# Windowed attention beside a gated scan: normalizing after the value product, reciprocals through the matrix engine, norms for two chunks together

## The chip, the cores and the metric

The kernel runs on one core of a Trainium2 chip. A core has five engines that each work through their own instructions in order and meet at semaphores: TensorE (PE; its weight loads are shown as PEld), VectorE (DVE), ScalarE (ACT), GpSimd (POOL) and SyncE (SP), which here issues most transfers between the device memory and SBUF. Matmul results land in PSUM, which is divided into banks of 512 float32 per partition. The metric is the device time of one execution in microseconds (us); the time shown of the kernel before is the median of three executions. A trace of one further execution was taken by the hardware profiler.

## The reference

One layer of a diffusion backbone: 1024 latent tokens (16 rows of 64) and 256 context tokens, width 1024. After a modulated RMS norm, one input projection feeds two groups:

- group A, a gated DeltaNet with 4 heads of 128, scanned forward and backward in chunks (the kernel takes chunks of 128: 2 of context, then 8 of latent tokens in each direction), then a per-head RMS norm and a gate;
- group B, neighbourhood attention with 8 heads of 64, each latent query over a window of latent keys and all context keys with one softmax.

Both are joined by an output projection, and a SwiGLU feed-forward follows. What the change touches is this much of it:

```python
# group B
s = jnp.concatenate([s_win.reshape(B, H, N_COL_BLK, QB_W, n_win), s_ctx], axis=-1)
p = jax.nn.softmax(s, axis=-1).astype(v.dtype)
o = (jnp.einsum("bhnqic,binchd->bnqhd", p_win, v_r)
     + jnp.einsum("bhnqk,bkhd->bnqhd", p[..., n_win:], v_ctx))
# group A, o_f and o_b from the two scans
o = (o_f + rev(o_b)).transpose(0, 2, 1, 3)
o = rms_norm(o, out_norm_w) * jax.nn.silu(z.astype(jnp.float32))
```

## The kernel before, in words

The kernel runs stage after stage: the modulation, the input projection (with the preparation of the scans' small inverses beside it), then **one stage in which the scans of group A and the attention of group B run interleaved**, then the output projection, the feed-forward's up products (L1313) and its down products (L1654). The change lies in the interleaved stage.

**Attention.** The work is 32 pairs: 4 head pairs (`hp`) x 2 halves of the rows x 4 column blocks. `pair` (L285) handles one: 128 queries of two heads (u = 0, 1) against 640 keys each. It takes a PSUM tile `sc` of three banks, of which two exist, so pair n+2 takes the one of pair n. Step one: the scores (L302, float16 high and low parts, 6 matmuls for u = 0 and 4 for u = 1); VectorE adds the bias tile `bt` and takes the row maximum (L304), negates it (L306), ScalarE takes the exponential with the maximum as bias and sums along the row (L307), VectorE takes the reciprocal of the sum (L308) and scales the 640 probabilities (L309). Step two: 5 transposes per head into `sc` (L314), copied out by ScalarE (L317). Step three: 10 matmuls with the values into columns 1280 to 1407 of `sc` (L324), the two heads on the two halves of the 128 output partitions, each 64 columns of the array; ScalarE copies the product to `out` (L326). `bt` is filled by POOL (zeros for the context, L270) and by a transfer issued on SP (L271), one pair ahead. Each complete `out` is split into a high and a low part by `store` (L365: ScalarE, then POOL L372).

**Scan.** `scan` (L1161) handles one chunk of one direction: matmuls with the state (L1171, L1181), with the inverse (L1190), the attention inside the chunk (L1202) and the state update (L1207), each followed by VectorE or ScalarE work on its result (L1173, L1184, L1187, L1194, L1196, L1203, L1213). Both directions run side by side, 10 rounds. The second direction to reach a latent chunk adds into `oacc` and then runs `finish(c)` (L1222) as the end of its own scan: load z, square sums on ScalarE (L1228), 14 small VectorE operations for the inverse root, four products with z and the root on VectorE (L1235), and, two rounds of its generator later, the transposes of the chunk (`turned`: L1111, L1114, L1115). The chunks that are last in their direction are transposed after the stage, behind the first output-projection matmuls.

**Order.** The work is written as generators. After each step of a live scan generator, `beside(PACE)` (L1246) gives the attention 0.72 of a step. A scheduler then orders each engine's instructions from that program, so matmuls of scan and attention alternate in small groups; on the chip each engine keeps this order. Instructions on different engines that touch the same PSUM bank are kept apart by semaphores.

Of the kernel before, what the change touches and what calls it, by code (L numbers as in the profile page):

```python
# [9 lines left out]
F32 = mybir.dt.float32  # L10
# [3 lines left out]
AF = mybir.ActivationFunctionType  # L14
OP = mybir.AluOpType
# [7 lines left out]
NAH, ND = 8, 64  # L23
# [65 lines left out]
def hybrid(ctx, tc, a, dbg):  # L89
# [37 lines left out]
    ident = M[C_ID]  # L127
# [125 lines left out]
    def attention(nw):  # L253

        def load(hd):
            qs = nw.tile([128, L], F16, name="qs", tag="qs", bufs=4)
            kh = nw.tile([128, T], F16, name="kh", tag="kh", bufs=4)
            kl = nw.tile([128, T], F16, name="kl", tag="kl", bufs=4)
            sp.dma_start(qs, nq_d[hd].rearrange("i d t -> (i d) t"))
            for i in range(2):  # L260
                sp.dma_start(kh[i * 64:i * 64 + 64], nk_d[0, hd])
                sp.dma_start(kl[i * 64:i * 64 + 64], nk_d[1, hd])
            return qs, kh, kl

        def biases(hp, half, cb):

            out = []
            for u, w0 in enumerate(WIN):
                bt = nw.tile([128, 640], F32, name="bt", tag="bt", bufs=4)
                pool.memset(bt[:, CTX[w0]], 0.0)  # L270
                sp.dma_start(bt[:, w0:w0 + 384], a["rpb"][2 * hp + u, half, CASE[cb]])  # L271
                out.append(bt)
            return out

        def values(hp, half, cb):
            vw = nw.tile([128, 3, 128], F32, name="vw", tag="vw", bufs=3)
            sp.dma_start(vw, vw_d[:, hp, cb, half:half + 3])
            return vw

        def context(hp):  # L280
            vc = nw.tile([128, 2, 128], F32, name="vc", tag="vc")
            sp.dma_start(vc, nv_d[0:CT, hp * 128:hp * 128 + 128].rearrange("(c p) d -> p c d", p=128))
            return vc

        def pair(heads, bts, vw, vc, half, cb, out):  # L285

            r0 = 4 * half
            sc = psum[-1].tile([128, 1536], F32, name="sc", tag="sc", bufs=2)
            mx = nw.tile([128, 2, 4], F32, name="mx", tag="mx", bufs=3)
            for u, (head, w0, bt) in enumerate(zip(heads, WIN, bts)):  # L290
                qs, kh, kl = head
                q = qs[:, (half * 4 + cb) * 128:(half * 4 + cb + 1) * 128]
                kv = [kx[:, CT:].rearrange("p (r c) -> p r c", c=64)[:, r0:r0 + 12, BLKS[cb]:BLKS[cb] + 32]
                      for kx in (kh, kl)]
                parts = [(CTX[w0].start, CTX[w0].stop, (kh[:, 0:CT], kl[:, 0:CT]))]
                if w0:
                    parts += [(256, 512, [x[:, 0:8] for x in kv]), (512, 640, [x[:, 8:12] for x in kv])]
                else:
                    parts += [(0, 384, kv)]
                for n0, n1, ks in parts:  # L300
                    for i in range(2):
                        pe.matmul(sc[:, u * 640 + n0:u * 640 + n1], q, ks[i], start=i == 0, stop=i == 1)  # L302
                m = mx[:, u]
                dve.tensor_tensor_reduce(bt, sc[:, u * 640:u * 640 + 640], bt, 1.0, -3.0e38, OP.add, OP.max,  # L304
                                         m[:, 0:1])
                dve.tensor_scalar(m[:, 1:2], m[:, 0:1], -1.0, None, op0=OP.mult)  # L306
                act.activation(bt, bt, AF.Exp, bias=m[:, 1:2], accum_out=m[:, 2:3])  # L307
                dve.reciprocal(m[:, 3:4], m[:, 2:3])  # L308
                dve.tensor_scalar(bt, bt, m[:, 3:4], None, op0=OP.mult)  # L309
            yield 1  # L310
            pts = []
            for u, bt in enumerate(bts):
                for j in range(5):
                    pe.transpose(sc[:, u * 640 + j * 128:u * 640 + (j + 1) * 128],  # L314
                                 bt[:, j * 128:(j + 1) * 128], ident)
                pt = nw.tile([128, 640], F32, name="pt", tag="pt", bufs=3)
                act.copy(pt, sc[:, u * 640:u * 640 + 640])  # L317
                pts.append(pt)
            yield 1
            for j in range(5):  # L320
                for u, (w0, pt) in enumerate(zip(WIN, pts)):
                    vals = [vc[:, i] for i in range(2)] + [vw[:, i] for i in range(3)]
                    vv = (vals[j] if w0 else vals[(j + 2) % 5])[:, u * ND:u * ND + ND]
                    pe.matmul(sc[u * ND:u * ND + ND, 1280:1408], vv, pt[:, j * 128:(j + 1) * 128],  # L324
                              start=j == 0, stop=j == 4)
            act.copy(out.rearrange("p (r b c) -> p r b c", r=8, b=4)[:, :, cb],  # L326
                     sc[:, 1280:1408].rearrange("p (r c) -> p r c", r=8))
            yield 1

        order = [(hp, half, cb) for hp in range(NAH // 2) for half in range(2) for cb in range(4)]  # L330
        heads = {0: [load(0), load(1)]}
        vcs = {0: context(0)}
        bt, vw = biases(*order[0]), values(*order[0])
        yield 1
        old = None
        for n, (hp, half, cb) in enumerate(order):
            if half == 1 and cb in (0, 2) and hp + 1 < NAH // 2:
                heads.setdefault(hp + 1, []).append(load(2 * hp + 2 + cb // 2))
                if cb == 0:
                    vcs[hp + 1] = context(hp + 1)  # L340
            if cb == 0:
                out = nw.tile([128, 512], F32, name="no", tag="no")
            if old:
                next(old)
            cur = pair(heads[hp], bt, vw, vcs[hp], half, cb, out)
            next(cur)
            if n + 1 < len(order):
                bt, vw = biases(*order[n + 1]), values(*order[n + 1])
            yield 1
            if old:  # L350
                next(old)
                if cb == 0:
                    store(*done)
            if cb == 3:
                done = out, hp, half
            old = cur
            yield 1
        next(old)
        yield 1
        next(old)  # L360
        store(*done)
# [755 lines left out]
    with ExitStack() as gs:  # L1117
# [10 lines left out]
        def work(name, bufs=2, dt=F32):  # L1128
            return sw.tile([128, 4, 128], dt, name=name, tag=name, bufs=bufs)
# [31 lines left out]
        def scan(d, c):  # L1161
# [52 lines left out]
                                                 op0=OP.mult, op1=OP.add)  # L1214
                S[d] = sn
            yield 1
            if lat:
                if c in seen:
                    yield from finish(c)
                seen.add(c)  # L1220

        def finish(c):  # L1222
            o = oacc[:, c - 2]
            z, sq = work("z"), work("sq", 1)
            sp.dma_start(fl(z), z_d[(c - 2) * 128:(c - 1) * 128])
            r = sw.tile([128, 4], F32, name="orr", tag="orr")
            for h in range(4):
                act.activation(sq[:, h], o[:, h], AF.Square, accum_out=r[:, h:h + 1])  # L1228
            t = sw.tile([128, 3, 4], F32, name="nwt", tag="nwt")
            dve.tensor_tensor(r, r, RQ2[:, c - 2], OP.mult)  # L1230
            dve.tensor_scalar(t[:, 0], r, 1.0 / DH, EPS, op0=OP.mult, op1=OP.add)
            rsqrt(r, t[:, 0], t[:, 1])
            dve.tensor_tensor(r, r, RQ[:, c - 2], OP.mult)
            for h in range(4):
                dve.scalar_tensor_tensor(o[:, h], o[:, h], r[:, h:h + 1], z[:, h], op0=OP.mult, op1=OP.mult)  # L1235
            if c in last:
                return
            yield 1
            yield 1
            turned(c)  # L1240
            yield 1

        last = [ORDER[0][-1], ORDER[1][-1]]
        count = [0.0]

        def beside(n):  # L1246
            count[0] += n
# [6 lines left out]
        for i in range(NCH):  # L1254
            if i + 1 < NCH:
                for d in range(2):
                    load(d, ORDER[d][i + 1], ORDER[1 - d][i + 2:i + 3])
            live = [scan(d, ORDER[d][i]) for d in range(2)]
            while live:
                nxt = []  # L1260
                for n, g in enumerate(live):
                    if next(g, 0):
                        nxt.append(g)
                    beside(PACE)
                live = nxt
        for _ in fill:
            pass

# [467 lines left out]
```

## Time and profile before

| | |
|---|---|
| time, median of 3 (lowest to highest) | 1556.46 us (1555.35 to 1559.38) |
| profiled execution: its own time | 1557.82 us |
| profiled execution: span from the first to the last instruction | 1556.0 us |
| granted TensorE clock, mean | 0.986 |
| busy PE, DVE, ACT, POOL, share of the span | 95%, 65%, 46%, 15% |
| instructions PE, DVE, ACT, POOL | 8702, 1856, 1376, 280 |
| scan-and-attention stage | about 577 to 823 us |

Busy times are sums over an engine's instructions. Matmuls overlap in the pipeline, so a busy TensorE may still lose time between them. A row of waits names the instruction that waited, what released it, and how long the engine stood idle for it in total, how often, and the longest. A row of groups gives line, engine, operation, tile written and read, shapes and count, then busy us and mean ns of one, then the engine's idle time before them and its releasers. A row of windows gives the busy us of each engine in a stretch, with the granted clock, the share of the DMA engines and their rate.

### The profile page before, as it was taken

How to read it: one execution, taken by the hardware profiler on the slowest of the kernel's cores; microseconds unless marked ns; L12 is line 12 of the kernel's file. 1: busy time of each engine (PE TensorE's matmuls, PEld its weight loads, DVE VectorE, ACT ScalarE, POOL GpSimd, SP SyncE). 2: the span in 40 equal slices, each digit the busy share in tenths (PEclk: the TensorE clock that was granted, in tenths of full speed). 3: DMA queues.
4: the chain of work that ended last, by engine and by line, in shares of the span. 5: the costliest groups of instructions: out<-in, count | busy, mean ns of one | idle time of the engine just before them, and what ended most of it. 6: DMA issues, size and time to landing. Idle time of an engine off the chain costs nothing. (4 is left out here: it accounts for less than half of the span.)

```text
span 1556.0 us, 24056 instructions
## 1 busy us (share of the span) xinstructions
PE 1481.6 (95%) x8702; PEld 1234.4 (79%) x8702; DVE 1003.7 (65%) x1856; ACT 718.5 (46%) x1376; POOL 229.1 (15%) x280
## 2 busy tenths in 40 slices
PE   7999999999889988997999999999999999999998
PEld 4788787679888766886788878888888888888887
DVE  5774496573254655678997559855665656689652
ACT  6442554654353355666763266333333334454440
POOL 1154401633354320111100000000000000000000
PEclk9999999999999999999999999999999999999999
DMA  9274221677355568999736601633323224698742
GB/s 391 59 221 125 72 76 61 204 219 212 122 173 157 167 190 251 283 287 262 213 114 227 233 34 53 227 108 106 104 102 102 102 102 156 229 378 283 241 147 81
DMA packets 202422, 267.35 MB, mean 172 GB/s; under 512 B 16832, under 2 KB 112576, under 8 KB 201280
## 3 DMA queue, kind: packets, MB, share of 16 engines
q1 hardware_dynamic: 196688, 261.07, 52.3%
q10 hardware_dynamic: 5616, 4.76, 0.9%
q8 instruction: 68, 1.11, 0.3%
q14 instruction: 50, 0.41, 0.1%
HBM read 201.02 MB, written 68.94 MB: 173 GB/s over the span
## 5 line engine op out<-in xcount | busy, mean ns | idle before, releaser
L403 PE MATMUL blk<-hh,whi 128*128 128x512 f32 (+1 forms) x410 | 122.4, 393 | 1.4 <-ACT kk L548 1.4
L1374 ACT CAST uhi<-wq 128x512 fp32r<-128x512 f32 x101 | 61.1, 622 | 132.2 <-issue 84.9
L1374 ACT CAST uhi<-ws 128x512 fp32r<-128x512 f32 x91 | 53.9, 621 | 146.7 <-PE ps L1313 92.5
L403 PE MATMUL blk<-hh,wlo 128*128 128x512 f32 (+1 forms) x410 | 117.0, 379 | 0.6 <-POOL wlo L200 0.6
L403 PE MATMUL blk<-hl,whi 128*128 128x512 f32 (+1 forms) x410 | 115.3, 376 | 0.3 <-DVE hl L689 0.3
L1375 DVE TENSOR_TENSOR ulo<-wq,uhi 128x512 fp32r<-128x512 f32 x101 | 67.6, 687 | 58.8 <-ACT uhi L1374 33.7
L1313 PE MATMUL ps<-hT,uhi 128*128 128x512 f32 x336 | 103.7, 390 | 0.0
L1313 PE MATMUL ps<-lT,uhi 128*128 128x512 f32 x336 | 103.5, 389 | 0.0
L1313 PE MATMUL ps<-hT,ulo 128*128 128x512 f32 x336 | 103.4, 389 | 0.0
L1313 PE MATMUL ps<-hB,uhi 128*128 128x512 f32 x288 | 89.2, 391 | 0.6 <-ACT hB L1488 0.6
L1313 PE MATMUL ps<-lB,uhi 128*128 128x512 f32 x288 | 88.8, 389 | 0.4 <-DVE lB L1489 0.4
L1313 PE MATMUL ps<-hB,ulo 128*128 128x512 f32 x288 | 88.6, 389 | 0.0
L586 PE MATMUL blk<-zhi,hh 128*128 128x256 f32 (+1 forms) x288 | 84.7, 294 | 1.1 <-ACT kk L548 1.1
L403 PEld LDWEIGHTS blk<-hh,wlo 128*128 128x128 f32 x410 | 72.5, 192 | 15.6 <-POOL wlo L200 0.9
L403 PEld LDWEIGHTS blk<-hl,whi 128*128 128x128 f32 x410 | 72.5, 193 | 14.8 <-DVE hl L689 0.8
L586 PE MATMUL blk<-zhi,hl 128*128 128x256 f32 (+1 forms) x288 | 83.0, 288 | 0.0
L403 PEld LDWEIGHTS blk<-hh,whi 128*128 128x128 f32 x410 | 69.9, 194 | 16.5 <-issue 4.0
L586 PE MATMUL blk<-zlo,hh 128*128 128x256 f32 (+1 forms) x288 | 81.8, 284 | 0.0
L1313 PEld LDWEIGHTS ps<-lT,uhi 128*128 128x128 f32 x336 | 63.1, 188 | 13.2
L1313 PEld LDWEIGHTS ps<-hT,ulo 128*128 128x128 f32 x336 | 63.1, 188 | 13.1
L1313 PEld LDWEIGHTS ps<-hT,uhi 128*128 128x128 f32 x336 | 62.9, 188 | 12.9
L200 POOL TENSOR_TENSOR wlo<-wraw,whi 128x1024 fp32r<-128x1024 f32 x18 | 44.7, 2484 | 183.8 <-ACT whi L199 164.4
(359 smaller groups left out, 3651.6 us busy)
## 6 DMA issues: line engine op xcount, KB each, us to landing
wq<-w_fo SPq DMA_DIRECT2D x99, 256.0 KB, 4.1
wq<-w_gu SPq DMA_DIRECT2D x88, 256.0 KB, 2.9
wad<-wa SPq DMA_DIRECT2D x64, 256.0 KB, 4.0
bt<-rpb SPq DMA_DIRECT2D x64, 192.0 KB, 3.6
t_d<-g SPq DMA_DIRECT2D x22, 512.0 KB, 3.6
fr<-t_d SPq DMA_DIRECT2D x44, 256.0 KB, 5.1
f_d<-g SPq DMA_DIRECT2D x33, 256.0 KB, 2.1
fr<-f_d SPq DMA_DIRECT2D x33, 256.0 KB, 4.3
```

Of the source, the lines that this page charges most:

```text
L200: lo_engine.tensor_tensor(o, r, h.bitcast(F32), OP.subtract)
L403: pe.matmul(o, ww[:, k], xx[k][:, s], start=k == 0 and j == 0, stop=k == KT - 1 and j == 2)
L586: pe.matmul(p[:, :c1 - c0], x[k][:, s], ww[:, k, c0:c1], start=k == 0 and j == 0, stop=k == KT - 1 and j == 2)
L1313: pe.matmul(o, w[wi][:, k], x[xi][:, k], start=first and k == 0 and j == 0, stop=k == n - 1 and j == 2, skip_group_check=True)
L1374: act.copy(hi, self.raw[key])
L1375: dve.tensor_tensor(lo, self.raw[key], hi.bitcast(F32), OP.subtract)
```

## The change

- **Softmax.** L304 now forms minus (score + bias) and takes the row minimum (the built-in factor is -1), so that the exponential is taken with scale -1 and that minimum as bias, and the negation L306 is gone. The probabilities stay undivided (L309 is gone); one reciprocal per pair covers both heads.
- **The division** comes after the product with the values. Two matmuls per pair, 64 columns wide, take the reciprocals (broadcast along the 64 columns) as weights and the identity as the moving operand, which turns them into rows that lie like the product, in columns 1408 to 1535 of `sc`. ScalarE copies them to `out`, and VectorE multiplies the product from PSUM into `out`, in place of ScalarE's copy L326.
- **The gated norm.** `finish` takes both chunks that ended in a round, and runs as a third generator beside the scans of the next round (after the last round, alone). The small operations work on both chunks at once; except for the last two chunks, POOL multiplies `oacc` with z, and ScalarE scales by the root in place of VectorE's L1235.

```diff
                 m = mx[:, u]
-                dve.tensor_tensor_reduce(bt, sc[:, u * 640:u * 640 + 640], bt, 1.0, -3.0e38, OP.add, OP.max,
+                dve.tensor_tensor_reduce(bt, sc[:, u * 640:u * 640 + 640], bt, -1.0, 3.0e38, OP.add, OP.min,
                                          m[:, 0:1])
-                dve.tensor_scalar(m[:, 1:2], m[:, 0:1], -1.0, None, op0=OP.mult)
-                act.activation(bt, bt, AF.Exp, bias=m[:, 1:2], accum_out=m[:, 2:3])
-                dve.reciprocal(m[:, 3:4], m[:, 2:3])
-                dve.tensor_scalar(bt, bt, m[:, 3:4], None, op0=OP.mult)
+                act.activation(bt, bt, AF.Exp, scale=-1.0, bias=m[:, 0:1], accum_out=m[:, 2:3])
+            dve.reciprocal(mx[:, :, 3], mx[:, :, 2])
             yield 1
...
             yield 1
+            for u in range(2):
+                pe.matmul(sc[u * ND:u * ND + ND, 1408:1536], mx[:, u, 3:4].to_broadcast([128, ND]), ident,
+                          start=True, stop=True)
+            o, av, inv = [x.rearrange("p (r c) -> p r c", r=8) for x in (out, sc[:, 1280:1408], sc[:, 1408:1536])]
+            o = o[:, :, cb * 16:cb * 16 + 16]
+            act.copy(o, inv)
             for j in range(5):
...
-            act.copy(out.rearrange("p (r b c) -> p r b c", r=8, b=4)[:, :, cb],
-                     sc[:, 1280:1408].rearrange("p (r c) -> p r c", r=8))
+            dve.tensor_tensor(o, av, o, OP.mult)
...
-            if lat:
-                if c in seen:
-                    yield from finish(c)
+            if c in seen:
+                ended.append(c)
+            elif lat:
                 seen.add(c)
 
+        def finish(cs):
+            cs = sorted(cs)
+            two = slice(cs[0] - 2, cs[1] - 1, cs[1] - cs[0])
+            os, zs = [oacc[:, c - 2] for c in cs], [work("z") for c in cs]
+            r = sw.tile([128, 2, 4], F32, name="orr", tag="orr")
+            for i, c in enumerate(cs):
+                sp.dma_start(fl(zs[i]), z_d[(c - 2) * 128:(c - 1) * 128])
+                sq = work("sq", 1)
+                for h in range(4):
+                    act.activation(sq[:, h], os[i][:, h], AF.Square, accum_out=r[:, i, h:h + 1])
+            final = cs == sorted(last)
+            if not final:
+                for o, z in zip(os, zs):
+                    pool.tensor_tensor(z, o, z, OP.mult)
+            yield 1
+            t = sw.tile([128, 3, 2, 4], F32, name="nwt", tag="nwt")
+            dve.tensor_tensor(r, r, RQ2[:, two], OP.mult)
             dve.tensor_scalar(t[:, 0], r, 1.0 / DH, EPS, op0=OP.mult, op1=OP.add)
             rsqrt(r, t[:, 0], t[:, 1])
+            dve.tensor_tensor(r, r, RQ[:, two], OP.mult)
+            for i, c in enumerate(cs):
+                for h in range(4):
+                    if final:
+                        dve.scalar_tensor_tensor(os[i][:, h], os[i][:, h], r[:, i, h:h + 1], zs[i][:, h],
+                                                 op0=OP.mult, op1=OP.mult)
+                    else:
+                        act.activation(os[i][:, h], zs[i][:, h], AF.Copy, scale=r[:, i, h:h + 1])
+                yield 1
+            for c in cs:
+                if c not in last:
+                    yield 1
+                    turned(c)
...
-            live = [scan(d, ORDER[d][i]) for d in range(2)]
+            live = [scan(d, ORDER[d][i]) for d in range(2)] + [finish(ended)] * bool(ended)
+            ended = []
...
+        run(finish(ended))
```

The body of the old `finish`, which this replaces, stands in the kernel before (L1222 to L1241).

More of the change, by code (lines that the diff above doesn't have):

```diff
@@ L1216, in scan @@
             yield 1
-            if lat:
-                if c in seen:
-                    yield from finish(c)
+            if c in seen:
+                ended.append(c)
+            elif lat:
                 seen.add(c)
[L1222 to L1230, printed above, removed]
+        def finish(cs):
[15 more added lines that the diff above has]
+            dve.tensor_tensor(r, r, RQ2[:, two], OP.mult)
@@ L1231, in finish @@
             dve.tensor_scalar(t[:, 0], r, 1.0 / DH, EPS, op0=OP.mult, op1=OP.add)
             rsqrt(r, t[:, 0], t[:, 1])
[L1233 to L1241, printed above, removed]
+            dve.tensor_tensor(r, r, RQ[:, two], OP.mult)
@@ L1243, in hybrid @@
         last = [ORDER[0][-1], ORDER[1][-1]]
-        count = [0.0]
+        count, ended = [0.0], []
         def beside(n):
```

## The prediction

> **What bounds the kernel now.** I read the page first (busy shares, chain), then cut the stage that the change touches out of the trace with the windows, then the waits of TensorE in it, then its groups and two stretches of the timeline.
>
> From the page, and from the chain in order of time:
>
> ```profile
> PE 1481.6 (95%) x8702; PEld 1234.4 (79%) x8702; DVE 1003.7 (65%) x1856; ACT 718.5 (46%) x1376; POOL 229.1 (15%) x280
> PE 40%; DVE 1%; issue 0%; DVEq 0%
> 927.18 320.97 PE ps L1313 x1416
> ```
>
> TensorE is busy 95% of the span, and from 927 us on the chain is TensorE alone: nothing there can take up or give back time, so what the scan-and-attention stage gains or loses reaches the end one to one. That stage starts with L302 and ends with the last L324, about 577 to 823 us:
>
> ```profile
> 577.00:823.00 246.00, 220.15 (x2018) 187.19 (x2017) 185.28 (x644) 160.10 (x416) 27.02 (x66) 0.99 0.77 231
> 740.00:760.00 20.00, 19.59 (x189) 17.45 (x190) 17.13 (x58) 13.76 (x39) 2.78 (x6) 1.00 0.79 232
> 760.00:780.00 20.00, 18.20 (x174) 14.31 (x174) 19.09 (x81) 14.40 (x35) 3.65 (x8) 1.00 0.67 191
> ```
>
> Columns: window, length, busy PE, PEld, DVE, ACT, POOL, granted clock, DMA share, GB/s. TensorE is busy 220 of 246 us, VectorE 185, ScalarE 160. Even where VectorE is busy 19.09 of 20 us, TensorE keeps 18.2. So TensorE leads the stage, and VectorE matters only through the stops it causes there. These stops, in the same window:
>
> ```profile
> PE sc L314 <- DVE bt L309: 4.6, 2, 4.1
> PE sc L302 <- ACT no L326: 4.5, 9, 1.5
> PE sc L302 <- DVE mx L304: 4.0, 6, 1.0
> PE sc L324 <- ACT pt L317: 3.0, 7, 0.8
> PE sc L314 <- DVE nwt L183: 1.6, 1, 1.6
> PE ps L1111 <- DVE oacc L1235: 1.4, 2, 0.9
> PEld L302 <- issue: 13.8, 29, 1.7
> PEld sc L314 <- issue: 10.0, 18, 4.5
> ```
>
> (waiting line, releaser: us in total, times, longest). Few stops show on the matmul row, because a matmul's record is 0.27 us long while the next starts 0.11 us after it:
>
> ```profile
> 653.08 0.27 PE L314 MATMUL sc<-cst,bt 128*128 128x128 f32 x1
> 653.19 0.27 PE L302 MATMUL sc<-kh,qs 128*128 128x256 f16 x1
> ```
>
> On the weight row the same stops are longer and more frequent (10.0 us in 18 at the transposes L314). I take the truth to lie between the two rows.
>
> **The change part by part.** There are 32 pairs (64 softmax halves, 32 products). Durations:
>
> ```profile
> L309 DVE TENSOR_SCALAR bt<-bt,mx 128x640 f32<-128x640 f32 x64 | 35.6, 556 | 0.6
> L308 DVE RECIPROCAL mx<-mx 128x1 f32<-128x1 f32 x64 | 10.2, 159 | 8.6 <-ACT bt L307 8.2
> L306 DVE TENSOR_SCALAR mx<-mx 128x1 f32<-128x1 f32 x64 | 9.2, 147 | 0.4
> L307 ACT ACTIVATE bt<-bt,mx 128x640 f32<-128x640 f32 x64 | 53.2, 831 | 28.3 <-DVE mx L306 13.6 <-issue 9.8 <-DVE nwt L183 1.8
> L1194 ACT ACTIVATE vk<-ps,KN 128x128 f32<-128x128 f32 x64 | 18.8, 377 | 2.2 <-PE ps L1190 1.8
> L326 ACT COPY no<-sc 128x128 f32<-128x128 f32 x32 | 8.5, 265 | 18.2 <-PE sc L324 17.7
> L1173 DVE SCALAR_TENSOR_TENSOR vn<-ps,EG,v 128x128 f32<-128x128 f32 x72 | 22.2, 342 | 4.4 <-PE ps L1171 4.2
> L1203 DVE TENSOR_TENSOR oacc<-ps,oacc 128x512 f32<-128x512 f32 x16 | 11.0, 687 | 5.7 <-PE ps L1202 5.6
> L1235 DVE SCALAR_TENSOR_TENSOR oacc<-oacc,orr,z 128x128 f32<-128x128 f32 x24 | 6.8, 344 | 0.3 <-DVE mx L308 0.3
> L182 DVE TENSOR_TENSOR nwt<-orr 128x4 f32<-128x4 f32 x18 | 2.7, 156 | 0.0
> L1228 ACT ACTIVATE sq<-oacc 128x128 f32<-128x128 f32 x29 | 8.6, 299 | 2.5 <-DVE oacc L1203 2.5
> L372 POOL TENSOR_TENSOR na<-no,na 128x512 fp32r<-128x512 f32 x6 | 7.9, 1316 | 16.2 <-ACT na L371 16.2
> ```
>
> (1) Softmax without division and negation. VectorE loses L309 (35.6 us), L306 (9.2) and half of the reciprocals (32 of 159 ns: 5.1). On the path from scores to transposes this is 0.56 + 0.16 + 0.15 = 0.86 us per half, with two hand-overs between VectorE and ScalarE less. It is worth only what TensorE stopped for: 4.6 + 4.0 + 1.6 = 10.2 us on the matmul row (L304 is late where VectorE is busy with the removed work). The lower end is 4 us (the one start-up stop of 4.1, if other delays fill the rest), the upper 18 (the weight row's 10.0 for L314, of L302's 13.8 the 4.0 in 8.5 that belong to VectorE, and L183's 1.6). I take -11, next to the matmul row. What is late next at the transposes is the exponential itself (831 ns on ScalarE).
>
> (2) Reciprocals turned on TensorE, the price. Two matmuls per pair, 64 columns wide like L324's and in two passes like those; the timeline at one product block:
>
> ```profile
> 650.33 0.30 PE L314 MATMUL sc<-cst,bt 128*128 128x128 f32 x1 [0.49 <-DVE bt L309]
> 650.55 0.32 PE L324 MATMUL sc<-pt,vc 128*64 128x128 f32 x1
> 650.56 0.32 PE L324 MATMUL sc<-pt,vw 128*64 128x128 f32 x1
> 650.71 0.27 PE L324 MATMUL sc<-pt,vc 128*64 128x128 f32 x1
> ...
> 650.82 0.27 PE L324 MATMUL sc<-pt,vc 128*64 128x128 f32 x1
> ...
> 651.59 0.27 PE L324 MATMUL sc<-pt,vc 128*64 128x128 f32 x1
> 651.80 0.33 PE L314 MATMUL sc<-cst,bt 128*128 128x128 f32 x1
> ```
>
> The two halves run side by side. Entering costs 0.22 us from the last full-width start, the second passes follow 0.16 later, and a full-width matmul starts 0.21 after the last pass: 0.59, less the 0.11 that stood there anyway, is 0.48 per pair, 15 us in all. If entering and leaving fall into waits, two passes of 0.11 are left: 7 us. In the built order the block stands apart from L324's in 31 of 32 pairs, so it mostly pays both; I take 0.40, +13 us. The Trainium skill has the rule behind it (TensorEngine Tiling (Array Packing), Key Properties): changing the tile mode, not only the tile, drains the engine. It gives no figure; the trace agrees with 0.21 to 0.22 in place of 0.11.
>
> (3) The new wait. The block writes the bank in which the product will lie; ScalarE copies it to `o`, and in the built program the first product matmul of all 32 pairs now waits for that copy (before, it waited for the copy of the transposes, which the block now waits for in its place). Queued behind it are all later TensorE work, the scan's too. Served at once, the copy ends about 0.55 us after the last pass (0.27 latency, 0.265 copy). Full-width work placed between, at 0.11 a pass, is 0.89 us in the mean and short of 0.55 in 12 pairs, by 2 us together: the lower end. ScalarE works in order, though, and 1.6 us of exponentials (831 ns) and evictions (377) stand ahead of the copy in the mean; if TensorE comes early each time, that makes 22 us: the upper end. The nearest row is the same copy in the old place, L302 <- L326, 4.5 us in 9 stops with 1.08 us of filler, hidden part not counted. I take +8. In the Trainium skill (PSUM — Partial Sum Buffer, PSUM bank collisions raise a hardware error) two engines have to be kept apart by bank and quadrant, not by address. The row L302 <- L304 above is such a wait, since the two touch different columns. If only overlapping columns had to wait, this term would be 0 and the sum 8 us lower; the built program decides against that.
>
> (4) The product's multiplication moves to VectorE: 32 of 128x128 from PSUM, not in the trace; between L182's 0.16 and L1203's 0.69, taken as L1173's 0.34: 11 us on VectorE, whose total still falls to about 130 us. It frees the score buffer as L326 did, in a shorter queue: 0, within 2 either way.
>
> (5) Gated norms of two chunks at once, a round later, beside the next round's scans. Per chunk 14 small VectorE operations of 0.156 become 14 for two chunks (-9 us of VectorE), 24 of 32 L1235 (0.344, -8 us) become 24 ScalarE scalings (0.30, +7 us of ScalarE) and 6 POOL products (1.3 each, +8 us of POOL). On TensorE's path lies only L1111 <- L1235, 1.4 us: -2. The other side: two POOL products (2.6 us) stand ahead of the memsets of the next bias tiles, and the z loads on SP, which need both buffers, stand ahead of bias and scan loads: at most +3; I keep -4 to +3. The last two chunks stay on VectorE, and the 48 output-projection matmuls cover them as now.
>
> (6) The start. The clock drops after the longest stop:
>
> ```profile
> 584.00:588.00 4.00, 1.09 (x5) 0.78 (x5) 3.60 (x11) 2.88 (x6) 0.00 (x0) 0.88 0.38 87
> 588.00:592.00 4.00, 3.22 (x18) 2.35 (x19) 2.08 (x6) 2.31 (x4) 0.83 (x2) 0.50 0.89 222
> 592.00:596.00 4.00, 2.83 (x27) 2.37 (x24) 1.20 (x5) 1.78 (x4) 0.31 (x1) 0.76 0.92 328
> ```
>
> That costs 4 x (0.12 + 0.50 + 0.24) = 3.4 us. The first exponential no longer waits behind a normalization on VectorE, so the stop shrinks, but TensorE stays sparse there: I take -1.5, between 0 and -3.4.
>
> Sum: -11 + 13 + 8 + 0 - 2 - 1.5 = +6.5. The profiled execution took 1557.8 us (1556.0 span and 1.8 around it), 1.4 above the median of 1556.5; so 1557.8 + 6.5 - 1.4 = 1563 us.
>
> **The rivals.** Faster: VectorE's lateness costs more than the matmul row shows. For it speak the weight rows and 19.09 of 20 us at 760; against it, that TensorE is no idler there than its mean (18.2 of 20 against 17.9). With (1) at -18, (3) at +2, (5) at -4, (6) at -3.4: -10.4, 1546 us. With the other terms as taken it begins where (1) passes -17.5.
>
> No change: (3) near 3, (1) near -13: 1556 us. Nothing in the rows excludes it.
>
> ScalarE becomes the bound: the copy sits behind exponentials in most pairs, +22 in (3): +20.5, 1577 us. Against it: ScalarE is busy only 160 of 246 us, and of 32 old copies only 9 stopped TensorE visibly.
>
> The change doesn't do what it says, since TensorE leads the stage anyway: (1) at -4, +13.5, 1570 us; I count it to the forecast's side.
>
> **How the numbers follow.** Forecast (with the 1570 case) 0.36, ScalarE as the bound 0.10, no change 0.24, faster 0.30. About 0.3% (4.7 us) is what can be told from none: faster 0.30, same 0.24, slower 0.46. Eight in ten reach from a little beyond the faster rival to a little short of the ScalarE one: 1543 to 1574; the forecast's own range is 1558 to 1570.
>
> **What would show it.** Right: the new matmuls' line with about 0.4 us per pair; a wait of the product on ScalarE's copy of 5 us or more; L314's waits on VectorE gone; VectorE near 130 us in the stage, and the stage longer by some 6 us. Wrong: the product hardly waits for the copy, or the waits at L302 and L314 fall by more than 18 us; then the stage ends before 815. A clock of 1.0 from 588 on would show (6) at its full size.

## The result: 0.31% slower, and the profile after

The changed kernel took 1560.92 us in the median of 11 executions (1558.99 to 1566.89), the kernel before 1555.98 us on the same chips. The ratio is 1.0031 with a 95% interval of 1.0017 to 1.0045: 4.8 us slower (2.6 to 7.0). The forecast was 1563 us and slower.

The page of the changed kernel first: busy times, and from its chain in order of time the long piece of the feed-forward that stood at 927.18 us before.

```profile
PE 1491.8 (96%) x8830; PEld 1240.2 (80%) x8830; DVE 964.3 (62%) x1648; ACT 723.9 (46%) x1400; POOL 235.7 (15%) x286
929.76 320.97 PE ps L1330 x1416
```

The piece is as long as before to the hundredth (320.97 us) and starts 2.6 us later; the pieces behind it on the chain are also as long as before, so what the chain lost lies ahead of it. (The two profiled spans differ by 3.4 us; the remaining 0.8 us lies behind the last work on the chain.) From the start of the first score matmul to that of the first output-projection matmul (below: the stage) the trace has 245.8 us against 241.9; the stage began 1.4 us earlier.

The windows of the changed kernel, the whole stage and its beginning; columns as before (window, length, busy PE, PEld, DVE, ACT, POOL, granted clock, DMA share, GB/s):

```profile
575.00:827.00 252.00, 235.25 (x2152) 196.90 (x2153) 150.35 (x457) 167.72 (x448) 36.37 (x74) 0.98 0.73 225
580.00:584.00 4.00, 1.34 (x9) 0.85 (x7) 3.33 (x7) 3.45 (x7) 0.00 (x0) 0.92 0.18 64
584.00:588.00 4.00, 2.44 (x13) 1.59 (x11) 1.54 (x4) 2.35 (x5) 0.62 (x2) 0.50 0.65 149
588.00:592.00 4.00, 3.87 (x28) 2.54 (x25) 0.02 (x1) 0.67 (x3) 0.00 (x0) 0.50 0.90 278
592.00:596.00 4.00, 3.17 (x20) 2.20 (x19) 1.93 (x6) 2.61 (x6) 0.47 (x2) 0.80 0.93 326
```

VectorE fell from 185 to 150 us, and the stage still grew: VectorE's busy time did not set its length. The clock, forecast to stay higher at the start, is at half through two of these windows where it was through one; summed as length times one less the granted clock, the loss is 5.1 us where it was 3.4.

TensorE's stops in the stage, first at the matmuls, then at the weight loads (waiting line, releaser: us in total, times, longest):

```profile
PE sc L319 <- ACT pt L315: 3.6, 4, 1.1
PE sc L312 <- DVE mx L304: 3.2, 2, 2.1
PE sc L328 <- ACT no L323: 3.0, 5, 1.8
PE sc L302 <- DVE mx L304: 1.0, 2, 0.6
PE sc L302 <- DVE no L330: 0.9, 2, 0.5
...
PEld sc L319 <- ACT pt L315: 6.9, 10, 1.3
PEld sc L328 <- ACT no L323: 5.0, 10, 2.0
```

The transposes (L312, before L314) no longer wait for a division; most of what is left there on the matmul row is the wait for the minimum that L304 now takes. New are the block L319, which waits for the eviction of the transposes in the product's place, and the product L328, which waits for ScalarE's copy of the reciprocals. The stops on VectorE and ScalarE that stood in the prediction's list for L314 and L302 (4.6, 4.5, 4.0, 1.6) are down to 3.2, 1.0 and 0.9.

The groups that the change made:

```profile
L306 ACT ACTIVATE bt<-bt,mx 128x640 f32<-128x640 f32 x64 | 53.1, 829 | 27.2 <-DVE mx L304 26.8
L307 DVE RECIPROCAL mx<-mx 128x2 f32<-128x2 f32 x32 | 5.3, 165 | 11.6 <-ACT bt L306 11.6
L319 PE MATMUL sc<-cst,mx 128*64 128x128 f32 x128 | 14.3, 302 | 3.9 <-ACT pt L315 3.6
L323 ACT COPY no<-sc 128x128 f32<-128x128 f32 x32 | 8.5, 265 | 5.6 <-PE sc L319 5.6
L330 DVE TENSOR_TENSOR no<-sc,no 128x128 f32<-128x128 f32 x32 | 9.3, 290 | 24.5 <-PE sc L328 23.6 <-ACT sq L1234 0.2
L1251 ACT ACTIVATE oacc<-z,orr 128x128 f32<-128x128 f32 x24 | 8.3, 404 | 0.0
L1238 POOL TENSOR_TENSOR z<-oacc,z 128x512 f32<-128x512 f32 x6 | 7.7, 1285 | 9.5 <-DVE oacc L1206 7.6 <-DMA z<-z_d 1.9
```

And one block in the timeline, between work of the scan and the transposes of the next pair:

```profile
649.57 0.72 PE L1193 MATMUL ps<-vn,y 128*128 128x128 f32 x5
650.22 0.44 PE L319 MATMUL sc<-cst,mx 128*64 128x128 f32 x4
650.59 0.66 PE L312 MATMUL sc<-cst,bt 128*128 128x128 f32 x4
```

The five L1193 start 0.11 apart, the last at 650.02 (650.22 less the 0.20 in the single starts of the trace). The two halves of the block start together, their second passes 0.17 later, and the transposes 0.20 after those: 0.57 us from one full-width start to the next, where 0.11 would stand without the block. In the trace, entering costs 0.20 to 0.22 in 21 of the 32 blocks, and leaving costs 0.20 or 0.21 in 28; the others took longer (up to 1.35 and 0.64 us).

### The profile page after: what moved, and what is told of

It reads as the page before. It is cut to its first block, busy times and chain, and to the rows that moved or that the text cites. A ratio compares the mean times of both kernels' runs of the same rounds, so it can differ in the third digit from the quotient of the medians.

```text
span 1559.4 us, 24085 instructions
## 1 busy us (share of the span) xinstructions
PE 1491.8 (96%) x8830; PEld 1240.2 (80%) x8830; DVE 964.3 (62%) x1648; ACT 723.9 (46%) x1400; POOL 235.7 (15%) x286
## 4 chain that ended last, share of the span: by engine, by line
PE 74%; DVE 9%; ACT 5%; DMA 4%; issue 3%; POOL 2%; SPq 1%; ACTq 0%; DVEq 0%; POOLq 0%
PE ps L1330 27%; PE ps L1671 13%; PE blk L406 7%; PE blk L589 5%; PE ps L1457 3%; PE sc L328 3%; PE sc L312 2%; PE sc L302 2%; PE ps L1307 1%; DVE N L872 1%; DVE tt L870 1%; PE pr L982 1%; PE ps L1174 1%; PE ps L1479 1%; PE ps L1193 1%
## 5 line engine op out<-in xcount | busy, mean ns | idle before, releaser
L304 DVE CUSTOM_DVE_ANT_0 bt<-sc,bt 128x640 f32<-128x640 f32 x64 | 52.6, 824 | 34.5 <-PE sc L302 17.0
```

## The experiments

Times are differences from the kernel before, ratio times 1556 us, with the 95% interval; two kernels are compared by their ratios. "Mode changes" are the places in the stage where a matmul of 64 columns follows one of 128 or the reverse, counted in the trace: 80 before, 142 after. The stage and the mode changes come from the one profiled execution of each kernel. It took about 3 us less than the kernel's median in e10 and e11, 2.3 less in e15, 3.2 more in e9 and 7.0 more in e14, so differences of stages are rough.

| kernel | ratio to before | us (95%) | stage, us | mode changes |
|---|---|---|---|---|
| changed kernel | 1.0031 | +4.8 (+2.6 to +7.0) | 245.8 | 142 |
| e1 softmax alone | 1.0064 | +10.0 (+6.2 to +13.5) | 253.4 | 144 |
| e2 norms alone | 0.9981 | -3.0 (-5.3 to -0.5) | 240.8 | 80 |
| e3 no division | 0.9920 | -12.4 (-15.1 to -9.8) | 229.8 | 96 |
| e9 block twice | 1.0058 | +9.0 (+7.2 to +11.0) | 250.8 | 144 |
| e5 block 128 wide | 0.9998 | -0.3 (-2.5 to +1.7) | 241.2 | 80 |
| e13 the same, spread by a copy | 0.9986 | -2.2 (-5.0 to +0.6) | 240.2 | 76 |
| e4 other bank | 1.0035 | +5.4 (+3.7 to +7.0) | 245.1 | 142 |
| e10 copy after | 1.0020 | +3.1 (+0.2 to +6.2) | 241.2 | 104 |
| e12 128 wide, copy after | 1.0021 | +3.3 (+0.6 to +5.9) | 245.6 | 102 |
| e15 128 wide, block early | 0.9959 | -6.4 (-9.6 to -3.3) | 234.6 | 90 |
| e11 norms, no negation | 1.0010 | +1.6 (-0.9 to +4.0) | 239.7 | 84 |
| e14 norm products on VectorE | 1.0047 | +7.3 (+4.4 to +10.1) | 247.6 | 144 |

The theory at the start was the prediction's sum: the softmax gains, its division's new place on TensorE costs more. The first rival was that the norms, with their work on ScalarE and GpSimd, carry the loss.

**e1 and e2: the two halves of the change.**

```diff
 # e1, against the changed kernel: the norms of the kernel before
-            if c in seen:
-                ended.append(c)
-            elif lat:
+            if lat:
+                if c in seen:
+                    yield from finish(c)
...
 # e2, against the changed kernel: pair() of the kernel before (L306 to L309, L326 as there)
```

> The attention of the changed kernel with the gated norms of the kernel before. Theory (the prediction's terms 1, 3, 4 and the price 2): the whole loss lies in the softmax part, and the norms give about 2 us: this kernel is 5 to 8 us slower than before, a little slower than the changed kernel. Rival (the loss comes from the norms: their scalings on ScalarE, the products on GpSimd, and a third piece of work per round): this kernel is within 2 us of before, or faster.

> The attention of the kernel before with the changed gated norms. Theory: 2 us faster than before (0 to 4), because the stop of the chunks' transposes L1111 on VectorE's last norm operation goes. Rival (the norms carry the loss): 4 us slower or more.

The softmax part alone costs 10 us (5 to 8 were expected, inside its interval of 6.2 to 13.5), the norms alone gain 3: the rival falls. Beside the new softmax the norms are worth 5.1 us (1.0031 against 1.0064), give or take 4, which their value alone does not contradict. The six executions of e1 spread from 1562 to 1572 us and its profile is of the slowest, so its stage of 253.4 us is not used further.

**e3: the softmax without its division.**

```diff
-            for u in range(2):
-                pe.matmul(sc[u * ND:u * ND + ND, 1408:1536], mx[:, u, 3:4].to_broadcast([128, ND]), ident,
-                          start=True, stop=True)
...
-            act.copy(o, inv)
...
-            dve.tensor_tensor(o, av, o, OP.mult)
+            dve.tensor_scalar(o, av, 1.0, None, op0=OP.mult)
```

> The changed kernel without the two reciprocal matmuls per pair and without ScalarE's copy of them; VectorE copies the product out without dividing, so this kernel leaves out the softmax's division altogether. It shows what the softmax chain alone gives, and with the changed kernel what the division's new place costs. Theory: the price of the block (13 us) and of the wait behind it (5 to 8 us) goes, so it is 16 to 21 us faster than the changed kernel, 11 to 16 faster than before. Rival (TensorE has slack that hides the block): at most 5 us faster than the changed kernel.

As the theory has it: 17.3 us by the ratios between this and the changed kernel (16.0 by the stages). TensorE has hardly any slack that would take up the block. Against e2, which has the same norms, the softmax without its work on VectorE gains 9.5 us, give or take 3.6 (11.0 by the stages). The stops show how (waits of TensorE in the stage, e2 and then e3):

```profile
PE sc L314 <- DVE bt L309: 5.5, 3, 4.1
PE sc L302 <- DVE mx L304: 5.3, 7, 1.0
PE sc L314 <- ACT pt L317: 3.8, 5, 1.5
PE sc L324 <- ACT pt L317: 3.8, 6, 1.0
PE sc L302 <- ACT no L326: 2.3, 3, 1.5
```

```profile
PE sc L324 <- ACT pt L315: 3.2, 4, 1.1
PE sc L302 <- DVE mx L304: 3.1, 4, 1.5
PE sc L312 <- DVE mx L304: 2.3, 2, 2.1
PE sc L312 <- ACT pt L315: 1.8, 4, 1.0
PE sc L302 <- DVE no L326: 0.9, 2, 0.5
```

The wait of the product on the eviction (L324, 3.2 us in e3) is about that of before (3.0); in the changed kernel the block has it (L319, 3.6), and the wait on the copy (L328, 3.0) comes on top.

**e9: the block twice, the price of the passes.**

```diff
             for u in range(2):
                 pe.matmul(sc[u * ND:u * ND + ND, 1408:1536], mx[:, u, 3:4].to_broadcast([128, ND]), ident,
                           start=True, stop=True)
+            for u in range(2):
+                pe.matmul(sc[u * ND:u * ND + ND, 1408:1536], mx[:, u, 3:4].to_broadcast([128, ND]), ident,
+                          start=True, stop=True)
```

> The changed kernel with the block of two reciprocal matmuls issued twice per pair; the second does the same work again right behind the first. It prices the passes without the change of mode and without a new wait. Theory (TensorE leads, two passes of 0.11 us per pair): 7 us slower than the changed kernel; up to 13 where the scheduler parts the two. Rival (TensorE has slack where the block stands): within 2 us of it.

4.2 us slower than the changed kernel (5.0 by the stages), give or take 2.9. Mode changes hardly grew (144), so the second block mostly stands behind the first. The 4.2 us are less than the 7 of the passes, but 7 lies at the edge of the interval: TensorE may have some slack there, or none.

**e5 and e13: one block matmul of 128 columns.**

```diff
 # e13; e5 has dve.reciprocal(rb, mx[:, :, 2:3].to_broadcast([128, 2, ND])) in place of the copy
+            rb = M[C_BD2].rearrange("p (u d) -> p u d", u=2)
+            dve.tensor_copy(rb, mx[:, :, 3:4].to_broadcast([128, 2, ND]))
             for u, bt in enumerate(bts):
...
-            for u in range(2):
-                pe.matmul(sc[u * ND:u * ND + ND, 1408:1536], mx[:, u, 3:4].to_broadcast([128, ND]), ident,
-                          start=True, stop=True)
+            pe.matmul(sc[:, 1408:1536], rb.rearrange("p u d -> p (u d)"), ident, start=True, stop=True)
```

> The changed kernel with one matmul 128 columns wide in place of the two 64 columns wide ones: VectorE writes the reciprocals already broadcast, 128x2x64, and the block needs no change of tile mode where it stands apart from the product. ScalarE's copy and the wait on it stay. Theory (changing the mode is about half of the block's price, 0.40 against two passes of 0.11): 5 to 6 us faster than the changed kernel. Rival (the changes of mode lie in waits that stand there anyway): within 2 us of it.

> The changed kernel with the 128-column block alone, its reciprocals spread by a plain copy on VectorE; ScalarE still copies the reciprocals ahead of the product. Against the one with the wide reciprocal it tells whether 25 us of VectorE's time in the stage matter. Theory (TensorE leads, VectorE has room): within 2 us of that one, 5 us faster than the changed kernel. Rival (VectorE's queue delays L304): 3 us faster than that one or more.

e5 is 5.1 us faster than the changed kernel, e13 7.0, each give or take 3 to 4, and the mode changes are back at 80 and 76. Where nothing waits, the block takes 0.34 us from one full-width start to the next in e13 (10 of the 32), 0.57 in the changed kernel (18 of the 32): 0.23 less, of which the two changes are 0.18 and the second pass, which follows after 0.11 instead of 0.17, about the rest. Over 32 pairs that makes at most 7.4 us. The price lies about as much in the changes of mode as in the passes. What VectorE spends on the spreading, from the groups of e5 and then of e13:

```profile
L309 DVE RECIPROCAL cst<-mx 128x128 f32<-128x128 f32 x32 | 30.4, 950 | 10.0 <-ACT bt L306 8.6 <-PE sc L313 1.4
```

```profile
L310 DVE COPY cst<-mx 128x128 f32<-128x128 f32 x32 | 9.0, 282 | 1.0
```

21 us less of VectorE, and the times differ by 1.9 us, give or take 3.5: VectorE has room, as the theory said, though a gain of 3 us, the rival's least, is not excluded.

**e4, e10 and e12: taking the wait away.**

```diff
 # e4, against the changed kernel
-                pe.matmul(sc[u * ND:u * ND + ND, 1408:1536], mx[:, u, 3:4].to_broadcast([128, ND]), ident,
+                pe.matmul(sc[u * ND:u * ND + ND, 0:128], mx[:, u, 3:4].to_broadcast([128, ND]), ident,
...
 # e10, against the changed kernel; e12 has this and the block of e13
-            act.copy(o, inv)
...
-            dve.tensor_tensor(o, av, o, OP.mult)
+            act.copy(o, av)
+            dve.tensor_tensor(o, inv, o, OP.mult)
```

> The changed kernel with the reciprocals turned into the first bank of the score buffer (columns 0 to 127, whose transposes have been copied out by then) in place of the bank of the product; the product's matmuls no longer wait for ScalarE's copy. It measures term 3 by itself. Theory (the wait costs what TensorE's stops at L328 show): 3 to 6 us faster than the changed kernel. Rival A (ScalarE's queue is the main loss): 8 us faster or more. Rival B (another wait comes late instead, the same copy at VectorE's multiplication and the next scores): within 2 us of the changed kernel.

> The changed kernel with the order of the two evictions turned round: ScalarE copies the product to out after it is done (as in the kernel before), and VectorE then multiplies it by the reciprocals straight from PSUM. No matmul waits for a copy of the reciprocals any more (in the built program the product then stands right behind the block and has no wait on ScalarE), so it takes term 3 away, and with it the second change of tile mode of term 2; the score buffer comes free later by one copy and a hand-over. Theory (the division's new place costs 16.6 us, of which the wait is 5 to 8 and the changes of mode 4 to 6): 9 to 13 us faster than the changed kernel, 4 to 8 faster than before. Rival A (the block's two passes themselves carry the loss): at most 5 us faster than the changed kernel. Rival B (the later freeing of the score buffer becomes the wait, at the scores L302): as slow as the changed kernel.

> Two repairs of the changed kernel together: one block matmul 128 columns wide (VectorE takes 128x2 reciprocals as in the changed kernel and spreads them with a plain copy, in place of the 950 ns of a reciprocal over 128x128), and ScalarE copies the product, which VectorE then multiplies by the reciprocals from PSUM. Theory (the change of mode, 5 us, and the wait, 2 to 4, are separate prices): 7 to 9 us faster than the changed kernel, 2 to 4 faster than before, like the norms alone or better. Rival (both repairs gave back the same stops, the one of e10 by the saved changes of mode alone): 4 to 5 us faster than the changed kernel, no different from before.

e4 tested nothing: in its built program all 32 products still wait for the copy, though it reads another bank, and in its trace none of the 32 starts less than 0.05 us after the copy's end. So the scheduler orders the score buffer as a whole here, not by its banks. Its expectation was wrong on what the edit does, and its time is that of the changed kernel.

In e10 the wait on the copy is gone and 38 of the mode changes with it, and it gains 1.7 us by the ratios (4.6 by the stages), not 9 to 13; give or take 3.7, it cannot be told from the changed kernel. By its time alone either rival fits, but the wait that rival B named, L302 on the freed buffer, is only 1.5 us (0.9 in the changed kernel). e12, which adds the 128-column block, is no faster than e10 and 1.6 us faster than the changed kernel, where the theory had 7 to 9 and the rival 4 to 5. It is 5.4 us (give or take 3.9) slower than e13, which keeps the copy in front. VectorE's waits suggest why; the changed kernel, then e10:

```profile
DVE no L330 <- PE sc L328: 23.6, 18, 6.4
DVE bt L304 <- PE sc L302: 17.0, 16, 3.6
...
DVE bt L304 <- issue: 7.5, 9, 2.1
```

```profile
DVE bt L304 <- issue: 15.8, 20, 2.6
DVE no L330 <- ACT no L329: 15.5, 11, 6.1
...
DVE bt L304 <- PE sc L302: 8.3, 7, 3.6
```

and TensorE's in e10:

```profile
PE sc L312 <- DVE mx L304: 4.5, 3, 2.2
PE sc L302 <- DVE mx L304: 3.2, 4, 1.4
PE sc L319 <- ACT pt L315: 2.2, 3, 0.8
```

The multiplication now waits for ScalarE's copy at the head of VectorE's queue, and the next L304 stands behind it. In the changed kernel L304 mostly waited for TensorE's scores (17.0 us; here 8.3), so here it comes late more often, and TensorE waits for it: 7.7 us where the changed kernel has 4.2. A wait has changed engines. This is read from one profile of each kernel, not tested by a run, and that it is all of the missing gain is not shown: e12's profile also has 3.4 us more lost to the clock than e13's.

**e15: the block early.** The two stops of a pair, block behind the eviction and product behind the copy, as one:

```diff
 # against e13
                 for j in range(5):
                     pe.transpose(sc[:, u * 640 + j * 128:u * 640 + (j + 1) * 128],
                                  bt[:, j * 128:(j + 1) * 128], ident)
+                if u:
+                    pe.matmul(sc[:, 0:128], rb.rearrange("p u d -> p (u d)"), ident, start=True, stop=True)
                 pt = nw.tile([128, 640], F32, name="pt", tag="pt", bufs=3)
                 act.copy(pt, sc[:, u * 640:u * 640 + 640])
                 pts.append(pt)
+            o, av, inv = [x.rearrange("p (r c) -> p r c", r=8) for x in (out, sc[:, 1280:1408], sc[:, 0:128])]
+            o = o[:, :, cb * 16:cb * 16 + 16]
+            act.copy(o, inv)
             yield 1
-            pe.matmul(sc[:, 1408:1536], rb.rearrange("p u d -> p (u d)"), ident, start=True, stop=True)
...
```

> The 128-column block spread by a plain copy, issued right behind the second head's transposes and ahead of their eviction, into the first bank of the score buffer; ScalarE copies the reciprocals right behind that eviction, one step of the attention before the product. In the built program the block then has no wait on ScalarE, and the product only the one for the copy of the reciprocals, so the two stops of each pair (block behind the eviction, product behind the copy) become one. Theory (each of the two stops costs TensorE what its row shows, 4.7 us and 3.8 us in the kernel with the block in its old place): the first goes, the second grows by less than 3 us, so 2 to 4 us faster than that kernel, 4 to 6 faster than before. Rival (the product waits as long in sum, now for both copies at once): within 2 us of that kernel.

1549.58 us in the median: 6.4 us (3.3 to 9.6) faster than before and 11.2 faster than the changed kernel. Against e13 it is 4.2 us faster by the ratios, give or take 4.2, which is hardly clear of the noise. Waits of TensorE in e13, matmuls, then in e15 (there the transposes are L314, the eviction L319, the block L317, the product L329):

```profile
PE sc L314 <- DVE mx L304: 3.4, 3, 2.1
PE sc L302 <- DVE mx L304: 2.6, 4, 1.0
PE sc L320 <- ACT pt L317: 2.2, 3, 0.8
PE ps L1210 <- DVE s L1216: 1.6, 1, 1.6
PE sc L328 <- ACT no L323: 1.3, 3, 0.5
PE ps L1193 <- DVE vn L1199: 1.3, 1, 1.3
PE sc L314 <- ACT pt L317: 1.0, 1, 1.0
```

```profile
PE sc L314 <- ACT pt L319: 4.4, 5, 1.8
PE sc L314 <- DVE mx L304: 2.5, 2, 2.1
PE sc L329 <- ACT no L323: 2.1, 3, 0.9
PE sc L302 <- DVE mx L304: 1.1, 3, 0.6
```

The block's wait (2.2 us on its row) is gone, the product's grew by 0.8, as the theory had it, but the second head's transposes wait 3.4 us longer for the eviction of the first, which lies in the same score buffer. Over the rows of the attention (`sc`) shown the sum falls only from 10.5 to 10.1 us. The gain shows elsewhere: TensorE's stops in the scan (L1210 and L1193 above, and smaller ones) fall from 4.8 to 0.5 us, and the profile of e15 lost 1.7 us less to the clock. All idle time on the matmul row in the stage falls from 18.4 to 13.5 us. That e15 is faster than before and than the changed kernel is shown; that merging the two stops is the reason is not, and why the scan's stops went was not tested.

**e11 and e14: parts of the change.**

```diff
 # e11, against e2
-                dve.tensor_tensor_reduce(bt, sc[:, u * 640:u * 640 + 640], bt, 1.0, -3.0e38, OP.add, OP.max,
+                dve.tensor_tensor_reduce(bt, sc[:, u * 640:u * 640 + 640], bt, -1.0, 3.0e38, OP.add, OP.min,
                                          m[:, 0:1])
-                dve.tensor_scalar(m[:, 1:2], m[:, 0:1], -1.0, None, op0=OP.mult)
-                act.activation(bt, bt, AF.Exp, bias=m[:, 1:2], accum_out=m[:, 2:3])
+                act.activation(bt, bt, AF.Exp, scale=-1.0, bias=m[:, 0:1], accum_out=m[:, 2:3])
...
 # e14, against the changed kernel
-            final = cs == sorted(last)
+            final = True
```

> The kernel before with the changed norms and without the negation (row minimum, exponential with scale -1), but with its division of the probabilities on VectorE. Theory (the chain from scores to transposes loses 0.15 us and no hand-over between engines, of 0.86 and two): 2 to 4 us faster than the norms alone, so 3 to 7 faster than before. Rival (VectorE's division, not the negation, sets every stop): no faster than the norms alone.

> The changed kernel with the norms of two chunks at once and a round later, but with the product with z and the root on VectorE for all chunks (as for the last two now), in place of GpSimd's products and ScalarE's scalings. The norms gave 6 us beside the new attention (2 forecast). Theory (VectorE's norm work stands ahead of L304, whose lateness is the first stop now): 2 to 4 us slower than the changed kernel. Rival (what gave the 6 us is that the norm runs a round later and off the scans' path, not whose engine does it): within 2 us of the changed kernel.

Without the negation but with the division, nothing is gained over e2 (4.5 us slower by the ratios, give or take 3.5, and 1.1 shorter by the stages; its executions spread from 1552 to 1566 us). Its waits of TensorE:

```profile
PE sc L313 <- DVE bt L308: 5.3, 5, 2.8
PE ps L1206 <- DVE vn L1195: 4.1, 3, 2.9
PE sc L313 <- DVE mx L307: 3.8, 1, 3.8
```

The transposes still wait for the division (L308, here with its reciprocal L307), and a stop in the scan (L1206) is new. So the rival of e11 stands, and why it is slower rather than equal stays open. e14 is 2.5 us slower than the changed kernel, where the theory had 2 to 4, but the intervals overlap: which engine does the norm's products is not settled.

## Why the prediction was right, by its own steps

The sign, the time (1560.9 against 1563, inside the forecast's own 1558 to 1570) and the reason hold: TensorE leads, the softmax gives less than its division's new place takes. The terms:

- **(1) and (4), softmax and multiplication, -11 and 0.** Together -9.5 by e3 against e2 (give or take 3.6). The split was off. On the matmul row TensorE's stops on the division and on L304 fall from 10.8 us in e2 (5.5 and 5.3) to 5.4 in e3 (2.3 and 3.1), about half of the 11, since L304 itself came late next at the transposes, where the prediction named the exponential. In the longest stop of the changed kernel the first half's exponential had ended at 582.07 us, and the transposes started at 583.47, when L304 of the second half, which reads the same score buffer, had ended (583.32). The rest came where nothing was booked: L302 waits for the freed buffer 0.9 us in e3 and 2.3 in e2, and the waits for ScalarE's eviction fell from 7.6 to 5.0 us. From before to the changed kernel the wait for the freed buffer fell from 4.5 to 0.9, but 2.2 of that comes with the norms alone (e2). Taking the negation alone out of the chain's 0.86 us gave nothing (e11).
- **VectorE "near 130 us"**: 150. The work went, in records: those of VectorE's operations in the stage sum to 225 us before and 173 after. But the busy time was 185 and is 150, since neighbouring records overlap and count once there. The prediction took means of records from a busy time in which they had counted less. The time did not depend on it.
- **(2) The block, +13.** The mechanism and the parts are as named: 0.20 to enter, 0.17 between the passes, 0.20 to leave. In the runs it was 4 to 5 for the passes (e9) and 5 to 7 for the mode changes and the closer second pass (e5, e13), 9 to 12 together, with 3 to 4 us of uncertainty on each. The rule of the Trainium skill that was named (TensorEngine Tiling (Array Packing), Key Properties: a change of mode drains the engine) agrees with the trace, which has 0.20 us in place of 0.11 at each change, 0.09 more each way.
- **(3) The new wait, +8.** It is there, but smaller: 3.0 us on the matmul row, 5.0 on the weight row, in the lower part of 2 to 22. It is not the product's wait alone that counts; the block has taken over the wait that the product had. Its reason was wrong: not the shared bank but the shared buffer makes the program wait (e4). The rule of the Trainium skill set beside it, that engines are kept apart by bank and quadrant (PSUM — Partial Sum Buffer, PSUM bank collisions raise a hardware error), was not put to the test by any run here, since the program's own order is stricter.
- **(5) Norms, -2.** -3.0 alone (0.5 to 5.3), in the range of -4 to +3. The transposes of the chunk (L1114, before L1111) no longer stop on the norm. Neither side effect that was feared shows among TensorE's stops.
- **(6) The start, -1.5.** It did not come. The longest stop fell from 4.1 to 2.1 us as said, and the clock still went to half: the windows lose 5.1 us where they lost 3.4, +1.7 in place of -1.5. The step that failed is "the stop shrinks, so the clock drops less". How far it is off is open, as one profile shows one execution: with the same longest stop of 2.1 us, e4, which runs like the changed kernel, lost 3.4 us at the start, and e15 1.7.

Of the signs that were named, the division's waits at L314 went and the block's price came as said. The product's wait reaches its 5 us only on the weight row, VectorE stayed at 150 us, and the stage of the profiles is 3.9 us longer, not 6.

From before by e2 and e3 to the changed kernel the steps are -3.0, -9.5 and +17.3, +4.8 in all. The forecast had -2, -11 and 21, and -1.5 for the start, which is inside these steps (the profiles of e2, e3 and the changed kernel lost 5.1, 3.4 and 5.1 us to the clock). So the division's place was taken 3.7 us too dear, the softmax and the start 1.5 us each too favourable, the norms 1.0 too small: errors that offset to 1.7. The sign and the order of the two large terms are shown; that the sum came within 2 us is partly luck, since the largest single error was 3.7 us and each step is uncertain by about 3.

Of the rivals, the faster one needed more than 17.5 from (1), against 9.5 here. No change needed (3) near 3 and (1) near -13: the first came close, the second did not (-9.5). ScalarE as the bound would have made the product's wait 22 us. That the softmax's gain stays hidden is excluded by e3.

## What to carry to other kernels

Where TensorE leads, work moved from VectorE to TensorE costs most of its price there (17.3 us here, of the 21 forecast). For narrow matmuls strewn among wide ones the change of mode was about as dear as the passes: one block of full width was 5 to 7 us faster. Taking a wait off one engine by letting another wait instead brought no gain clear of noise here (e10), and the profile shows TensorE waiting longer for that other engine. Doing the small work a step earlier, at full width, gave the fastest kernel that still divides (e15, 6.4 us faster than before), for a reason that the rows show only in part. Busy time of an engine that is not the bound is worth little by itself: 21 us less of VectorE, from e5 to e13, brought 1.9 us, inside the noise.

## What the runs showed of the hardware

- **The clock's loss comes in steps of 1.7 us.** Over the stage, windows of 4 us summed as length times one less the granted clock, it was 3.4 us before, 5.1 after, and 1.7, 3.4, 5.1 or 6.8 in the twelve other profiles: multiples of 3.4 us at half clock. The Trainium skill (TensorE: Matmul & The Clock Gate, What's actually happening) has a free-running window of about 3.4 us, and the steps agree. The table of the Trainium skill (TensorE: Matmul & The Clock Gate, Why this matters for your kernels) asks for no gaps above about 3 us. Here shorter ones were enough: in the changed kernel the longest stop ahead of the drop was 2.1 us, with TensorE busy 1.34 of the 4 us (580 to 584) at whose end the clock went to half; in e15 TensorE was busy 1.58 of the 3.4 us ahead of the drop (580.8 to 584.2), with no gap above 1.0 us inside them. In these traces the drop follows sparse work, not only a long gap.
- **A reciprocal over 128x128 on VectorE took 950 ns, a copy of the same shape 282, a reciprocal over 128x2 165** (e5, e13, the changed kernel).
- **Half-width matmuls: 0.20 us from a full-width start to a half-width one and 0.20 back**, against 0.11 between full-width ones.
